# Where the activations of a two-layer trunk lie in SBUF, and a paired up product in its first network

## The chip, the cores and the metric

The kernel runs on one core of a Trainium2 chip. The metric is the device time of one execution in microseconds, the median of several runs. All arithmetic is in 32-bit floats; large products split each operand into a high part, rounded to the format that TensorE multiplies in one pass (float32r), and a low part, the rest.

## The reference

A sequence of 256 tokens of width 2048 goes through two layers. Each layer is a token mixer and a gated network; each sub-layer is normalised, scaled and shifted by a modulation computed from a vector c, and added back through a gate.

```python
for i in range(DEPTH):
    shift, scale, gate = ada_ln(c, mix_mod_w[i], mix_mod_b[i])
    h = rms_norm(x, mix_norm_g[i]) * (1.0 + scale) + shift
    y = conformer_conv_module(h, ...) if i % 2 == 0 else stick_breaking_mixer(h, ...)
    x = x + gate * y
    shift, scale, gate = ada_ln(c, ffn_mod_w[i], ffn_mod_b[i])
    h = rms_norm(x, ffn_norm_g[i]) * (1.0 + scale) + shift
    x = x + gate * conv_ffn(h, ffn_up_w[i], ffn_dw_w[i], ffn_dw_b[i], ffn_down_w[i])
return rms_norm(x, final_norm_g)

def conv_ffn(h, up_w, dw_w, dw_b, down_w):
    u = causal_depthwise_conv(h @ up_w, dw_w, dw_b)   # width 3, 2 x 5632 channels
    gt, val = jnp.split(u, 2, axis=-1)
    return (jax.nn.silu(gt) * val) @ down_w
```

## The kernel before

Everything is kept transposed: channels on the 128 partitions, the 256 tokens along the free axis. A width of 2048 is thus 16 tiles of 128 x 256, the network's 5632 channels are 44. A product runs over weight blocks of 128 x 128; a column block (128 output channels) of an up product has 16 weight blocks, one of a down product 22 in each of its two halves. Eight weight blocks are a piece of 512 KB, loaded by SyncE's queue. For each piece ScalarE casts the weights to the high part `wh` (line 244) and VectorE subtracts to the low part `wl` (line 248). `look["split"]` is 3: this is done three pieces ahead of the piece that TensorE works on; `wh` and `wl` have four buffers each, `raw` six.

`gemm` (line 271 on) multiplies in one of two ways. Without `both`, a weight block takes three matmuls of 256 columns: `wh` by the operand's high half (304), `wh` by its low half (305), `wl` by its high half (306). With `both` it takes two: `wh` by high and low half together, 512 columns (299), and `wl` by the high half, 256 columns (300). The first of these leaves two partial sums side by side in PSUM, and whoever takes the result must add the halves.

The stages in order: convolution mixer (products pw1, pw2), first network (up00a, up00b, up01a, down00, up01b, down01), attention (qk, v, o), second network (the same names with a 1 first), final norm. A network's up product is cut in two halves, each followed by a down product over the 22 tiles that it has made; up00a, qk0a and up10a are the four column blocks with which a stage opens, on an operand that is not yet normalised, and never paired. Before the change, the products up10b, up11a, up11b, the later query and key products, all down products (but one column block each) and o are paired; up00b, up01a, up01b are not.

`up_done` takes each finished column block of an up product to `conv3`: ScalarE makes y, the last tap with its bias (line 1000), VectorE adds the two earlier taps (1003). With `both`, ScalarE first copies one half from PSUM (996) and VectorE adds the other (997). When gate and value of a channel tile are there, ScalarE takes the silu (1014), VectorE multiplies (1015), ScalarE casts the result to g's high half (1017), VectorE subtracts to its low half (1018). In `down_done` ScalarE scales one half (1024), GpSimd adds it to x (1025) and VectorE adds the other half (1029).

Beside the products runs the modulation. Rows of the modulation weights are loaded by GpSimd's queue (331) and reduced against silu(c) by VectorE (338). `tick`, called after each piece, spreads these steps by `RATES`: 0.4 a piece in up00b, 0.39 in the other up products of the first network, 0.43 in the down products. `Entry.add` scales x into a raw h as soon as a column block of x is done (458, 459), and `Rms.add` adds up squares, on GpSimd (406).

Tiles lie in SBUF in the order of their pools: constants, x, the 16 tiles of h, weight buffers, temporaries, modulation rows, and last what belongs to a stage (the convolution's tiles, z, g, or attention's with o). An h tile holds two halves of 264 floats (2112 bytes); the first h tile begins at byte 32,800 of each partition, which is 32 modulo 256. A g tile has 2304 bytes, its low half 1056 bytes behind the high one, and begins at 160 modulo 256; an o tile has 2176 bytes, so the o tiles begin at 160 and 32 in turn.

Of the kernel before, what the change touches and what calls it, by code (L numbers as in the profile page):

```python
# [26 lines left out]

PAIRS = {"z": (264, 528, 0), "g0": (264, 576, 0), "g1": (264, 576, 0), "o": (264, 544, 0)}
HEAD = 16
# [88 lines left out]
def hybrid_trunk(ctx: ExitStack, tc: tile.TileContext, cfg: Cfg, io: dict):  # L118
    nc = tc.nc
    D, T, H = cfg.D, cfg.T, cfg.H  # L120
    KD, KF, CW, FW = cfg.KD, cfg.KF, cfg.CW, cfg.FW
# [22 lines left out]
    def t256(name="t", bufs=6):  # L144
        return tmp.tile([P, T], F32, name=name, bufs=bufs)
# [10 lines left out]
    nc.vector.memset(ones_d, 1.0 / D)  # L156
    ones_q = const.tile([P, P], F32, name="ones_q")
    nc.vector.memset(ones_q, 1.0 / 32)
    ones = const.tile([P, P], F32, name="ones")
    nc.vector.memset(ones, 1.0)  # L160
    eps_r = const.tile([P, 1], F32, name="eps_r")
# [16 lines left out]
    fill = []  # L178
# [185 lines left out]
    HP = T + 8  # L364
    pairs = {}

    def h_tiles(i):
        v = hpool.tile([P, 2 * HP], F32R, name=f"h{i}")
        pairs[i] = v.rearrange("p (a t) -> p a t", a=2)[:, :, :T]
        return [v[:, a * HP:a * HP + T + 2] for a in range(2)]  # L370

    def h_pairs():
        return [pairs[k] for k in range(KD)]

    ahead_of = {kind: v[2] for kind, v in PAIRS.items()}

    def halved(pool, kind, name):

        low, size, _ = PAIRS[kind]
        at = ahead_of.pop(kind, 0)  # L380
        v = pool.tile([P, at + size], F32R, name=name)[:, at:at + 2 * low].rearrange("p (a t) -> p a t", a=2)[:, :, :T]
        return v[:, 0], v[:, 1], v
# [122 lines left out]
    with ExitStack() as cv:  # L505
# [12 lines left out]
        for k in range(0, D, 512):  # L518
            ps = psum_acc()
            nc.tensor.matmul(ps, ones[0:1, :], crow[0:1, k:k + 512], start=True, stop=True)  # L520
            nc.scalar.activation(csr[:, k:k + 512], ps, AF.Silu)
        rs = rms.rstd()
# [127 lines left out]
        for kt in range(KD):  # L650
# [5 lines left out]
        ident = homes_of_taps.pop()  # L656
        nc.gpsimd.affine_select(out=ident, in_=ones, pattern=[[1, P]], compare_op=ALU.is_equal, fill=0.0, base=0,
                                channel_multiplier=-1)
# [123 lines left out]
        def gather_copy(name):  # L782
            st["g" + name] = t256()
            nc.scalar.copy(st["g" + name], st[name][:, :T])

        def gather(name):

            nc.tensor.matmul(st[name][:, T:2 * T], ones_q, st.pop("g" + name), start=True, stop=name == "y0",
                             skip_group_check=True)
# [191 lines left out]
    def ffn(i, entry, out):  # L981
# [3 lines left out]
        with ExitStack() as fs:  # L985
# [6 lines left out]
            def conv3(ps, nb, both):  # L992
                y = t256()
                if both:
                    s = t256()
                    nc.scalar.copy(s, ps[:, T:2 * T])
                    nc.vector.tensor_tensor(s, ps[:, :T], s, op=ALU.add)
                    ps = s
# [90 lines left out]
    with ExitStack() as at:  # L1089
# [9 lines left out]
        ones_r = apool.tile([P, P], F32R, name="ones_r")  # L1099
        nc.scalar.copy(ones_r, ones)  # L1100

# [259 lines left out]
```

## Time and profile before

| | |
|---|---|
| median of 3 runs | 2296.48 us (2296.34 to 2298.68) |
| profiled execution | 2295.19 us |
| span of its instructions | 2293.5 us |
| granted TensorE clock | 0.998 |
| VectorE busy | 1790.7 us, 78% |
| ScalarE busy | 1218.8 us, 53% |
| GpSimd busy | 410.7 us, 18% |

The profile is of one execution. Its page gives the busy time of each engine, the clock in 40 slices, the chain of work that ended last, and the costliest groups of instructions; a group reads "line, engine, operation, output<-inputs, shapes, count | busy us, mean ns of one | idle us of the engine before them, and what ended it". The trace behind it can be asked for the same groups within a window, for busy time by window, for waits, and for instructions in order of time (start, duration, what). Matmuls overlap and their ends are modelled, so the time of one is read from the length of a stage divided by the number of its weight blocks.

### The profile page before, as it was taken

Reading aid. Unit: us, or ns where it says so; the run is one execution under the profiler, and the core shown is the slowest. Engines: PE = TensorE matmul, PEld = TensorE weight load, DVE = VectorE, ACT = ScalarE, POOL = GpSimd, SP = SyncE. Lnnn points to the kernel's source line nnn. Section 1 sums busy time; section 2 is a strip of 40 time slices with the busy share of each in tenths; the row PEclk is TensorE's granted clock in tenths of the full one; section 3 lists DMA queues with packets and bytes.
Section 4 is the critical chain, followed back from the end, with each engine's and each line's share of the span. In section 5 each row is a group of like instructions: output and inputs, shape, how many; then the busy total and the mean of one; then the engine's idle time right before and its main releaser. Section 6 shows DMA issues by size and latency. Waiting matters only on the chain.

```text
span 2293.5 us, 37839 instructions
## 1 busy us (share of the span) xinstructions
PE 2259.2 (99%) x14466; PEld 2011.7 (88%) x14466; DVE 1790.7 (78%) x2504; ACT 1218.8 (53%) x1930; POOL 410.7 (18%) x534
## 2 busy tenths in 40 slices
PE   7999999999999999999999999999999999999997
PEld 5888678999998999998898888888888888888887
DVE  7689968989998899999975555779899755777654
ACT  2056655755544455554465555657555544555553
POOL 4058713200003100003411100112000010000031
PEclk9999999999999999999999999999999999999999
DMA  9988798789899989888755555566777566656663
GB/s 397 417 336 305 273 363 349 290 298 337 332 350 340 338 329 340 336 333 307 277 185 159 165 174 169 170 189 235 240 282 277 193 191 188 190 185 186 192 192 111
DMA packets 139144, 603.16 MB, mean 263 GB/s; under 512 B 15441, under 2 KB 15569, under 8 KB 115153
## 3 DMA queue, kind: packets, MB, share of 16 engines
q1 hardware_dynamic: 120242, 464.42, 57.7%
q0 software_dynamic: 18720, 136.32, 16.0%
q8 instruction: 113, 1.85, 0.3%
q14 instruction: 69, 0.57, 0.1%
HBM read 598.58 MB, written 2.10 MB: 262 GB/s over the span
## 4 chain that ended last, share of the span: by engine, by line
PE 86%; DVE 7%; DMA 4%; ACT 1%; issue 1%; POOL 0%; DVEq 0%; SPq 0%; ACTq 0%; POOLq 0%
PE ps L299 32%; PE ps L300 16%; PE ps L304 9%; PE ps L305 9%; PE ps L306 8%; PE ps L694 5%; DMA mraw<-in_mt_mix 3%; DVE mraw L338 3%; DVE wl L248 2%; PE ps L1184 1%; PE ps L1185 1%; PE ps L1186 1%; PE ps L586 1%; DMA mraw<-in_mt_ffn 1%; DMA raw<-in_w_pw 1%
## 5 line engine op out<-in xcount | busy, mean ns | idle before, releaser
L248 DVE TENSOR_TENSOR wl<-raw,wh 128x1024 fp32r<-128x1024 f32 x688 | 848.0, 1239 | 299.5 <-ACT wh L244 297.7
L244 ACT CAST wh<-raw 128x1024 fp32r<-128x1024 f32 x688 | 719.0, 1047 | 660.6 <-PE ps L299 283.5
L299 PE MATMUL ps<-h,wh 128*128 128x512 f32 x1760 | 619.0, 394 | 0.0
L300 PE MATMUL ps<-h,wl 128*128 128x256 f32 x1760 | 494.0, 281 | 0.0
L299 PE MATMUL ps<-g,wh 128*128 128x512 f32 x1320 | 458.6, 393 | 0.0
L304 PE MATMUL ps<-h,wh 128*128 128x256 f32 (+1 forms) x1504 | 422.0, 281 | 0.0
L305 PE MATMUL ps<-h,wh 128*128 128x256 f32 (+1 forms) x1504 | 420.8, 280 | 0.0
L306 PE MATMUL ps<-h,wl 128*128 128x256 f32 (+1 forms) x1504 | 419.2, 279 | 0.1
L299 PEld LDWEIGHTS ps<-h,wh 128*128 128x128 f32 x1760 | 330.5, 188 | 74.5
L338 DVE CUSTOM_DVE_ANT_0 mraw<-mraw,csr 128x2048 f32<-128x2048 f32 x152 | 350.4, 2305 | 31.2 <-DMA mraw<-in_mt_mix 28.5
L300 PE MATMUL ps<-g,wl 128*128 128x256 f32 x1320 | 367.8, 279 | 2.3 <-DVE wl L248 2.2
L300 PEld LDWEIGHTS ps<-h,wl 128*128 128x128 f32 x1760 | 332.7, 189 | 0.2
L299 PEld LDWEIGHTS ps<-g,wh 128*128 128x128 f32 x1320 | 247.8, 188 | 57.8
L305 PEld LDWEIGHTS ps<-h,wh 128*128 128x128 f32 x1504 | 284.8, 189 | 0.1
L306 PEld LDWEIGHTS ps<-h,wl 128*128 128x128 f32 x1504 | 282.8, 188 | 0.7 <-DVE wl L248 0.7
L304 PEld LDWEIGHTS ps<-h,wh 128*128 128x128 f32 x1504 | 282.6, 188 | 0.1
L300 PEld LDWEIGHTS ps<-g,wl 128*128 128x128 f32 x1320 | 248.1, 188 | 4.1 <-DVE wl L248 4.1
L694 PE MATMUL ps<-h,raw 128*128 128x256 f32 x832 | 188.6, 382 | 0.0
L694 PEld LDWEIGHTS ps<-h,raw 128*128 128x128 f32 x832 | 158.0, 191 | 28.1 <-issue 5.8
L1025 POOL TENSOR_TENSOR x<-x,t 128x256 f32<-128x256 f32 x56 | 70.0, 1250 | 530.1 <-ACT t L1024 529.8
L1003 DVE SCALAR_TENSOR_TENSOR t<-t,par 128x254 f32<-128x254 f32 (+1 forms) x184 | 88.8, 483 | 46.6 <-ACT t L1000 43.7
L734 DVE SCALAR_TENSOR_TENSOR auxb<-u,cpar,auxb 128x256 f32<-128x256 f32 x297 | 121.6, 483 | 4.5 <-ACT auxb L718 3.7
(272 smaller groups left out, 2735.0 us busy)
## 6 DMA issues: line engine op xcount, KB each, us to landing
raw<-in_w_down SPq DMA_DIRECT2D x176, 512.0 KB, 4.3
mraw<-in_mt_ffn POOLq DMA_DIRECT2D x64, 1024.0 KB, 6.7
raw<-in_w_pw SPq DMA_DIRECT2D x96, 512.0 KB, 8.0
mraw<-in_mt_mix POOLq DMA_DIRECT2D x48, 1024.0 KB, 7.9
raw<-in_w_up01b SPq DMA_DIRECT2D x84, 512.0 KB, 6.8
raw<-in_w_up11b SPq DMA_DIRECT2D x84, 512.0 KB, 3.6
raw<-in_w_up00b SPq DMA_DIRECT2D x80, 512.0 KB, 6.1
raw<-in_w_up10b SPq DMA_DIRECT2D x80, 512.0 KB, 4.7
```

Source lines behind the costliest of these rows:

```text
L244: nc.scalar.copy(wh[:, :n], v[:, :n])
L248: nc.vector.tensor_tensor(wl[:, :n], v[:, :n], wh[:, :n].bitcast(F32), op=ALU.subtract)
L299: nc.tensor.matmul(o, wh[:, c], both[kt], start=first, stop=False, skip_group_check=True)
L300: nc.tensor.matmul(o[:, :T], wl[:, c], xh[kt], start=False, stop=left[nb] == 0, skip_group_check=True)
L304: nc.tensor.matmul(o, wh[:, c], xh[kt], start=first, stop=False, skip_group_check=halves > 0)
L305: nc.tensor.matmul(o, wh[:, c], xl[kt], start=False, stop=False, skip_group_check=halves > 0)
L306: nc.tensor.matmul(o, wl[:, c], xh[kt], start=False, stop=left[nb] == 0, skip_group_check=halves > 0)
L338: nc.vector.tensor_tensor_reduce(out=v, in0=v, in1=csr, scale=1.0, scalar=0.0, op0=ALU.mult, op1=ALU.add, accum_out=macc[:, nb:nb + 1])
L694: nc.tensor.matmul(banks[j][:, nb // KD * T:(nb // KD + 1) * T], w[:, b * P:(b + 1) * P], hf[kt], start=first, stop=left[j] == 0, skip_gro ...
L734: nc.vector.scalar_tensor_tensor(conv_ps[j], us[j % UBUFS][:, k:k + T], tap(j, k), conv_ps[j], op0=ALU.mult, op1=ALU.add)
L1003: nc.vector.scalar_tensor_tensor(y[:, s:], ps[:, :T - s], w(k), y[:, s:], op0=ALU.mult, op1=ALU.add)
L1025: nc.gpsimd.tensor_tensor(xs[nb], xs[nb], t, op=ALU.add)
```

## The change

- **h.** An h tile gets 2304 bytes (the last one 2176), and the first begins 128 bytes later. With the constants 1024 bytes shorter, the first h then begins at byte 31,904 and all of them at 160 modulo 256, their low halves still 1056 bytes further.
- **g of the first network, and o.** Halves of 1024 bytes without a gap, so that the 512 columns are one run; all of them begin at 64 modulo 256. The second network's g stays as it was.
- **The first network's up product** is paired, as the second's is. ScalarE copies all 512 columns of a finished block from PSUM to a new tile `e`, GpSimd adds the halves there, and y and the two taps read the sum from SBUF.
- **Room.** The constants 1/32 and 1 go: ScalarE multiplies by D or D/32 in operations that it already had, and GpSimd fills the identity with ones itself. The two tiles m1 and dm of the convolution take the slots of the temporaries `tm`.

```diff
-PAIRS = {"z": (264, 528, 0), "g0": (264, 576, 0), "g1": (264, 576, 0), "o": (264, 544, 0)}
+PAIRS = {"z": (264, 528, 0), "g0": (256, 512, 40), "g1": (264, 576, 0), "o": (256, 512, 40)}
+H_AHEAD, H_SIZE, H_LOW, H_LAST = 32, 576, 264, 544
...
-    ones_q = const.tile([P, P], F32, name="ones_q")
-    nc.vector.memset(ones_q, 1.0 / 32)
-    ones = const.tile([P, P], F32, name="ones")
-    nc.vector.memset(ones, 1.0)
...
     def h_tiles(i):
-        v = hpool.tile([P, 2 * HP], F32R, name=f"h{i}")
-        pairs[i] = v.rearrange("p (a t) -> p a t", a=2)[:, :, :T]
-        return [v[:, a * HP:a * HP + T + 2] for a in range(2)]
+        at = H_AHEAD if i == 0 else 0
+        v = hpool.tile([P, at + (H_LAST if i == KD - 1 else H_SIZE)], F32R, name=f"h{i}")
+        pairs[i] = bass.AP(tensor=v.tensor, offset=v.offset + at, ap=[list(v.ap[0]), [H_LOW, 2], [1, T]])
+        return [v[:, at + a * H_LOW:at + a * H_LOW + T + 2] for a in range(2)]
...
-        low, size, _ = PAIRS[kind]
-        at = ahead_of.pop(kind, 0)
-        v = pool.tile([P, at + size], F32R, name=name)[:, at:at + 2 * low].rearrange("p (a t) -> p a t", a=2)[:, :, :T]
+        low, size, ahead = PAIRS[kind]
+        at = ahead if foremost.setdefault(kind, name) == name else 0
+        v = pool.tile([P, at + size], F32R, name=name)
+        v = bass.AP(tensor=v.tensor, offset=v.offset + at, ap=[list(v.ap[0]), [low, 2], [1, T]])
         return v[:, 0], v[:, 1], v
...
-            nc.tensor.matmul(ps, ones[0:1, :], crow[0:1, k:k + 512], start=True, stop=True)
-            nc.scalar.activation(csr[:, k:k + 512], ps, AF.Silu)
+            nc.tensor.matmul(ps, ones_d[0:1, :], crow[0:1, k:k + 512], start=True, stop=True)
+            nc.scalar.activation(csr[:, k:k + 512], ps, AF.Silu, scale=float(D))
...
-        nc.gpsimd.affine_select(out=ident, in_=ones, pattern=[[1, P]], compare_op=ALU.is_equal, fill=0.0, base=0,
+        nc.gpsimd.memset(ident, 1.0)
+        nc.gpsimd.affine_select(out=ident, in_=ident, pattern=[[1, P]], compare_op=ALU.is_equal, fill=0.0, base=0,
...
-        m1 = cpool2.tile([P, T], F32, name="m1")
-        dm = cpool.tile([P, T], F32, name="dm")
+        m1 = t256("tm", 2)
+        dm = t256("tm", 2)
...
             def conv3(ps, nb, both):
                 y = t256()
-                if both:
+                if both and i == 0:
+                    s = gpool.tile([P, 2 * T], F32, name="e", bufs=2)
+                    nc.scalar.copy(s, ps)
+                    nc.gpsimd.tensor_tensor(s[:, :T], s[:, :T], s[:, T:], op=ALU.add)
+                    ps = s
+                elif both:
                     s = t256()
                     nc.scalar.copy(s, ps[:, T:2 * T])
                     nc.vector.tensor_tensor(s, ps[:, :T], s, op=ALU.add)
...
-            both = h_pairs() if i else None
-            rest = (lambda nb, ps: up_done(nb, ps, True)) if i else up_done
+            both = h_pairs()
+            rest = lambda nb, ps: up_done(nb, ps, True)
```

More of the change, by code (lines that the diff above doesn't have):

```diff
@@ L367, in h_tiles @@
     def h_tiles(i):
-        v = hpool.tile([P, 2 * HP], F32R, name=f"h{i}")
-        pairs[i] = v.rearrange("p (a t) -> p a t", a=2)[:, :, :T]
-        return [v[:, a * HP:a * HP + T + 2] for a in range(2)]
+        at = H_AHEAD if i == 0 else 0
+        v = hpool.tile([P, at + (H_LAST if i == KD - 1 else H_SIZE)], F32R, name=f"h{i}")
+        pairs[i] = bass.AP(tensor=v.tensor, offset=v.offset + at, ap=[list(v.ap[0]), [H_LOW, 2], [1, T]])
+        return [v[:, at + a * H_LOW:at + a * H_LOW + T + 2] for a in range(2)]
     def h_pairs():
         return [pairs[k] for k in range(KD)]
-    ahead_of = {kind: v[2] for kind, v in PAIRS.items()}
+    foremost = {}
     def halved(pool, kind, name):
-        low, size, _ = PAIRS[kind]
-        at = ahead_of.pop(kind, 0)
-        v = pool.tile([P, at + size], F32R, name=name)[:, at:at + 2 * low].rearrange("p (a t) -> p a t", a=2)[:, :, :T]
+        low, size, ahead = PAIRS[kind]
+        at = ahead if foremost.setdefault(kind, name) == name else 0
+        v = pool.tile([P, at + size], F32R, name=name)
+        v = bass.AP(tensor=v.tensor, offset=v.offset + at, ap=[list(v.ap[0]), [low, 2], [1, T]])
         return v[:, 0], v[:, 1], v
@@ L783, in gather_copy @@
             st["g" + name] = t256()
-            nc.scalar.copy(st["g" + name], st[name][:, :T])
+            nc.scalar.activation(st["g" + name], st[name][:, :T], AF.Copy, scale=D / 32.0)
         def gather(name):
-            nc.tensor.matmul(st[name][:, T:2 * T], ones_q, st.pop("g" + name), start=True, stop=name == "y0",
+            nc.tensor.matmul(st[name][:, T:2 * T], ones_d, st.pop("g" + name), start=True, stop=name == "y0",
                              skip_group_check=True)
@@ L1099, in hybrid_trunk @@
         ones_r = apool.tile([P, P], F32R, name="ones_r")
-        nc.scalar.copy(ones_r, ones)
+        nc.scalar.activation(ones_r, ones_d, AF.Copy, scale=float(D))
         def attention(h):
```

## The prediction

> **What bounds the kernel now.** I read the page's busy shares, clock and chain first, to see which engine sets the end.
>
> ```profile
> span 2293.5 us, 37839 instructions
> PE 2259.2 (99%) x14466; PEld 2011.7 (88%) x14466; DVE 1790.7 (78%) x2504; ACT 1218.8 (53%) x1930; POOL 410.7 (18%) x534
> PEclk9999999999999999999999999999999999999999
> PE 86%; DVE 7%; DMA 4%; ACT 1%; issue 1%; POOL 0%; DVEq 0%; SPq 0%; ACTq 0%; POOLq 0%
> ```
>
> TensorE is busy nearly all the time, at full clock, and is 86% of the chain. Two things can therefore move the end: the time of a matmul, and a weight that arrives late. So next I cut the span into the two networks' product stages (columns: length, then busy time and count of PE, weight loads, VectorE, ScalarE, GpSimd, then clock and DMA).
>
> ```profile
> 429.70:665.70 236.00, 235.60 (x2018) 235.40 (x2018) 219.69 (x293) 127.80 (x182) 15.18 (x29) 1.00 0.89 335
> 665.70:780.10 114.40, 114.40 (x663) 99.85 (x662) 98.08 (x98) 50.91 (x59) 28.25 (x32) 1.00 0.93 348
> 780.10:787.90 7.80, 7.80 (x69) 7.80 (x68) 6.58 (x7) 2.53 (x3) 0.53 (x1) 1.00 1.01 392
> 787.90:1023.10 235.20, 235.20 (x2019) 235.20 (x2018) 216.50 (x275) 123.21 (x180) 16.41 (x31) 1.00 0.89 332
> 1023.10:1141.80 118.70, 116.41 (x663) 100.36 (x662) 113.47 (x125) 60.37 (x90) 44.59 (x40) 1.00 0.81 295
> 1923.20:2158.40 235.20, 235.20 (x1347) 206.31 (x1346) 169.01 (x248) 133.63 (x206) 0.00 (x0) 1.00 0.61 188
> 2158.40:2272.80 114.40, 114.40 (x662) 99.86 (x661) 58.62 (x60) 62.48 (x88) 27.79 (x27) 1.00 0.55 167
> ```
>
> Rows 1 and 4 are the first network's up product (42 column blocks of 16 weight blocks each: 672), three matmuls of 256 columns per weight block. Row 6 is the second network's up product: 672 weight blocks too, but two matmuls, one of 512 columns and one of 256. Both take 235.2 us, 350.0 ns a weight block. **Pairing by itself saves no TensorE time.** Row 7 is a down product, also paired: 330 weight blocks in 114.4 us, 346.7 ns. The same two matmuls are 3.3 ns cheaper on g than on h.
>
> What differs is where the operand lies. Counting the tiles up as they are allocated, every g begins at byte 160 modulo 256 with its low half at 192. An h tile is 2112 bytes, so the h tiles begin in turn at 32, 96, 160 and 224 modulo 256. After the change every h begins at 160 with its low half at 192: the places that g has now.
>
> Unpaired, those places look no better: row 3 is a column block of g with three matmuls, 22 weight blocks in 7.8 us, 355 ns against 350 for h unpaired.
>
> **VectorE is the second limit in the first network only.** In rows 1 and 4 it is idle for 236.0 - 219.69 = 16.3 us and 235.2 - 216.50 = 18.7 us, together 35.0. In row 5, the second down product, it is at 113.47 of 118.7, and there TensorE needs 4.3 us more than the 114.4 of its siblings. The waits of that stage say on what:
>
> ```profile
> PEld ps L300 <- DVE wl L248: 4.1, 6, 1.0
> ```
>
> So a VectorE that is nearly full costs TensorE time, through the low halves of the weights.
>
> **The change, part by part.**
>
> *Placement of h.* Paired products on h gain 3.3 ns a weight block, taken from rows 6 and 7. Second network: 2 x 672 = 1344 blocks, 4.5 us. Attention's paired query and key products: 28 column blocks x 16 = 448, 1.5 us. The three stages that open on unpaired h (12 column blocks, 192 weight blocks) may lose as row 3 suggests: 192 x 5 ns = 0.9 at most, 0 at least; I take 0.5.
>
> *Pairing up 0.* 1344 blocks go from 350.0 to 346.7 ns: 4.5 us of TensorE time, if the weights keep up.
>
> *g of the first network and o.* They get halves of exactly 1024 bytes, one run of 512, beginning at 64 modulo 256. No operand of the trace has that place in a run of its own. The nearest rows are 6 and 7: between 346.7 and 350 ns, and not beyond, as both contain mixed and uniform places. With 660 paired blocks of g and 256 of o, that is 0 to 3 us of loss; a gain can't be excluded, since nothing shows that 160 is the best of all places: the same 3 us the other way. I take 0.
>
> *What follows a finished column block (84 times).* ScalarE copies 512 columns from PSUM, GpSimd adds the halves, ScalarE makes y from SBUF, VectorE's two taps read SBUF instead of PSUM.
>
> ```profile
> L1190 ACT COPY v<-ps 128x512 f32<-128x512 f32 x6 | 3.5, 587 | 4.1 <-PE ps L1186 3.7
> L1000 ACT ACTIVATE t<-t,par 128x256 f32<-128x256 f32 x92 | 55.3, 601 | 89.2 <-DVE t L997 89.1
> L1000 ACT ACTIVATE t<-ps,par 128x256 f32<-128x256 f32 x82 | 45.8, 558 | 0.0
> L1003 DVE SCALAR_TENSOR_TENSOR t<-t,par 128x254 f32<-128x254 f32 x92 | 44.3, 482 | 43.7 <-ACT t L1000 43.7
> L1003 DVE SCALAR_TENSOR_TENSOR t<-ps,par,t 128x254 f32<-128x254 f32 x82 | 39.1, 477 | 0.0
> L734 DVE SCALAR_TENSOR_TENSOR auxb<-u,cpar,auxb 128x256 f32<-128x256 f32 x297 | 121.6, 483 | 4.5 <-ACT auxb L718 3.7
> L869 POOL TENSOR_TENSOR y<-y,h 128x256 f32<-128x256 f32 x143 | 104.7, 732 | 13.3 <-ACT h L743 3.2
> L1025 POOL TENSOR_TENSOR x<-x,t 128x256 f32<-128x256 f32 x56 | 70.0, 1250 | 530.1 <-ACT t L1024 529.8
> ```
>
> ScalarE gets 84 x (587 + 601 - 558) = 53 us more on 251 busy of 471: it has room. VectorE's own operations stay as they are (482 against 477). GpSimd gets 84 adds of 0.73 us (L869) to 1.25 us (L1025), 61 to 105 us of 471, almost unused now. None of that is on the path by itself. The price is what the add does to VectorE:
>
> ```profile
> 719.97 1.78 POOL L1025 TENSOR_TENSOR x<-x,t 128x256 f32<-128x256 f32 x1 [2.36 <-ACT t L1024]
> 718.87 2.29 DVE L338 CUSTOM_DVE_ANT_0 mraw<-mraw,csr 128x2048 f32<-128x2048 f32 x1
> 721.08 1.75 DVE L248 TENSOR_TENSOR wl<-raw,wh 128x1024 fp32r<-128x1024 f32 x1
> ```
>
> The add starts inside L338, lasts 1.78 us instead of 0.73, and ends at 721.75; the split that VectorE starts at 721.08 takes 1.75 instead of 1.21 to 1.22. They take turns: the add waits for the running VectorE operation, and the next one waits 0.54 us for the add. It is not so for every pair: the adds of L869 run beside the convolution taps of L734, which have one operand in SBUF and one in PSUM, and neither is stretched (732 and 483). Split, reduction, product and, after the change, the taps of up 0 all read two operands from SBUF.
>
> The Trainium skill ("SBUF — State Buffer", Who interferes with whom) states this as a rule: a VectorE instruction with two SBUF inputs contends with a GpSimd one that reads SBUF, one with a single SBUF input does not. "Perfetto Trace Analysis" of the same skill (Optimizing Scalar/DVE Operations) warns that moving work between the two might not help. The trace agrees with the first; the second would come out as the first rival below.
>
> How often it happens is read from the same groups in stages with and without adds (first half of up 0, down 0, down 1, in this order):
>
> ```profile
> L248 DVE TENSOR_TENSOR wl<-raw,wh 128x1024 fp32r<-128x1024 f32 x85 | 102.9, 1221 | 13.8 <-ACT wh L244 13.1
> L338 DVE CUSTOM_DVE_ANT_0 mraw<-mraw,csr 128x2048 f32<-128x2048 f32 x29 | 66.2, 2284 | 0.0
> L248 DVE TENSOR_TENSOR wl<-raw,wh 128x1024 fp32r<-128x1024 f32 x42 | 52.8, 1271 | 9.9 <-ACT wh L244 9.9
> L338 DVE CUSTOM_DVE_ANT_0 mraw<-mraw,csr 128x2048 f32<-128x2048 f32 x18 | 41.8, 2322 | 0.0
> L248 DVE TENSOR_TENSOR wl<-raw,wh 128x1024 fp32r<-128x1024 f32 x42 | 57.4, 1378 | 2.2 <-ACT wh L244 2.2
> L338 DVE CUSTOM_DVE_ANT_0 mraw<-mraw,csr 128x2048 f32<-128x2048 f32 x17 | 39.7, 2338 | 0.0
> L459 DVE SCALAR_TENSOR_TENSOR h<-x,a_mix,h 128x256 fp32r<-128x256 f32 x14 | 12.5, 894 | 1.8 <-ACT h L458 1.8
> L1025 POOL TENSOR_TENSOR x<-x,t 128x256 f32<-128x256 f32 x14 | 22.5, 1605 | 22.1 <-ACT t L1024 22.0
> L406 POOL TENSOR_TENSOR sumsq<-sumsq,t 128x256 f32<-128x256 f32 x13 | 15.4, 1186 | 35.9 <-ACT t L402 35.9
> ```
>
> Down 0, VectorE 86% busy: 42 x 0.050 + 18 x 0.038 = 2.8 us over 14 adds, 0.20 us each. Down 1, 96% busy: 42 x 0.157 + 17 x 0.054 + 14 x (0.894 - 0.48) = 13.3 us over 27 adds, 0.49 us each. Up 0 stands at 93% before the adds, so it is nearest to the second: 84 x 0.49 = 41 us (17 and 45 are the ends, by 0.20 and by 0.54), against 35.0 us of idle time and 4.5 us less TensorE time. VectorE would come out 41 - 35 + 4.5 = 10.7 us too slow, about 5 us in each half.
>
> That is about what the pipeline can hide. A weight piece is split three pieces ahead, 8 blocks x 0.35 x 3 = 8.4 us; cast (row below) and subtraction take 1.05 and 1.22 of it, so VectorE can be some 6 us late. The lag of the first half is worked off in down 0 (114.4 - 98.08 = 16 us idle). That of the second enters down 1, which has 5.2 us idle and loses time already. I charge 2 us in up 0 (0 to the 17.5 of the rival) and 3 us in down 1 (0 to 5).
>
> ```profile
> L244 ACT CAST wh<-raw 128x1024 fp32r<-128x1024 f32 x688 | 719.0, 1047 | 660.6 <-PE ps L299 283.5
> ```
>
> *New waits.* ScalarE's y waits for the add, up to one VectorE operation of 2.3 us plus 0.73. Behind it stands the cast of the next piece, and behind that VectorE's subtraction; the 6 us of cover serve here too. The add in turn stands in GpSimd's queue behind the loads of modulation rows, which wait for the buffer that a reduction frees:
>
> ```profile
> POOL mraw L331 <- DVE macc L338: 70.6, 11, 13.9
> ```
>
> That buffer was reduced a step earlier in VectorE's order, so I cost it at nothing; if VectorE lags by a step, it is the rival's mechanism too. The removed constants, the rescaled ones, the identity's memset and m1 and dm in other slots lie beside stages that wait for transfers and reductions: 0.
>
> *Sum.* -4.5 - 1.5 + 0.5 - 4.5 + 0 + 2 + 3 = -5.0 us. The profiled execution took 2295.19, its span 2293.5 and 1.7 around it; that gives 2290.2. The median of the runs is 1.3 above the profiled one: 2291.5.
>
> **The rivals.**
>
> *VectorE becomes the bound (slower).* Each block's chain (copy, add that waits for VectorE, y, taps) leaves VectorE idle as well as locked out. For: down 1 shows 4.3 us lost per 114.4 with VectorE at 96%. Against: down 1 also carries h and the squares. Price: 4.3 x 471/114.4 = 17.7 us in up 0 in place of 2, so +11: 2307. It decides once an add costs VectorE over 0.14 us more than 0.49 (6 us of cover over 42 blocks).
>
> *The adds land in VectorE's idle time (faster).* For: the splits of row 1 wait 13.1 us for casts, and the add comes just behind a cast. At 0.20 us each, 17 us fit into 35. Then the 5 us of stalls go: 2286.5.
>
> *Placement does nothing.* The change would not do what it says: h's 350 ns comes from something else than its address, say the traffic of VectorE and ScalarE in those stages. Against: row 6 and row 7 differ although their VectorE shares are both low (72% and 51%), and row 1 gives 350 with another load. Then the gains of 10 are 0; VectorE is only 41 - 35 = 6 us too slow, and half of the stalls stays: 2299. The Trainium skill ("SBUF — State Buffer", Who interferes with whom) has TensorE never wait on anyone and names no rule of place; that is this case, and the 3.3 ns between g and h speak against it.
>
> **How the numbers follow.** About 0.2% is what a measurement here can tell from no change, 4.6 us. Forecast 0.40, its share on the faster side 0.25, within 0.15 (2291.5 lies at the bound); VectorE the bound 0.28, slower; adds hidden 0.15, faster; placement nothing 0.17, of it 0.13 within and 0.04 slower. Faster 0.40, same 0.28, slower 0.32. The range reaches from the hidden adds with a gain at g (2285) to VectorE as the bound (2308). As both signs hold much, the forecast's own range is 2288 to 2296.
>
> **What would show it.** Second network's up product: 232.9 to 233.1 us instead of 235.2; 235 says placement does nothing. First network's: 233 to 237 instead of 235.2 and 236.0, with VectorE over 98% busy, splits near 1.4 us and GpSimd adds of 1.1 to 1.8. Down 1: 119 to 124 instead of 118.7. If up 0 takes over 240 a half, with TensorE waiting for L248, the rival has it; if splits stay at 1.25, the adds are hidden.

## The result and the profile after

The changed kernel takes 2316.95 us (median of 4 runs, 2314.52 to 2318.45) against 2296.41 (4 runs, 2296.07 to 2298.68) measured beside it: a ratio of 1.0086, 95% interval 1.0073 to 1.0099. It is slower by 20.5 us, and outside the range that was given. Of e2, e3 and e10 below, one execution each ran at a granted clock of 0.66 to 0.85 and took 2475 us or more; without it the medians given there would be lower by 0.2, 0.2 and 0.8 us.

The profiled execution took 2317.71 us. Its page, for the whole span:

```profile
span 2316.0 us, 35321 instructions
PE 2263.1 (98%) x13122; PEld 1948.3 (84%) x13122; DVE 1819.8 (79%) x2502; ACT 1252.3 (54%) x2014; POOL 554.8 (24%) x619
PE 72%; DVE 16%; DMA 4%; issue 4%; ACT 2%; POOL 1%; DVEq 0%; SPq 0%; ACTq 0%; POOLq 0%
```

TensorE's share of the chain fell from 86% to 72%, VectorE's rose from 7% to 16%: the end now waits for VectorE in places. Where, the cut into stages says (columns as in the prediction; first and second half of the first network's up product, its two down products, then the two halves of the second network's up product):

```profile
433.20:679.40 246.20, 237.89 (x1346) 203.68 (x1345) 229.42 (x288) 143.44 (x221) 84.64 (x72) 1.00 0.88 315
803.20:1048.90 245.70, 237.83 (x1345) 203.44 (x1345) 227.00 (x268) 136.76 (x205) 85.93 (x73) 1.00 0.87 310
679.40:795.50 116.10, 114.75 (x663) 101.47 (x662) 103.29 (x103) 52.69 (x62) 32.01 (x35) 1.00 0.95 354
1048.90:1170.10 121.20, 117.62 (x663) 102.63 (x662) 117.75 (x132) 63.15 (x107) 48.14 (x42) 0.99 0.82 302
1592.00:1825.80 233.80, 233.25 (x1346) 203.46 (x1345) 209.43 (x309) 140.53 (x223) 6.88 (x13) 1.00 0.75 263
1948.00:2180.90 232.90, 232.90 (x1346) 203.31 (x1345) 168.91 (x248) 133.50 (x206) 0.00 (x0) 1.00 0.60 190
```

The second network gained what was expected: 232.9 us where it was 235.2, 346.6 ns a weight block. The first network's up product lost 10.2 and 10.5 us (246.2 and 245.7, from 236.0 and 235.2). Of the span's 22.5 us, up 0 makes 20.7, the two down products 1.7 and 2.5, the stages before the first network 3.5 (2.6 of it a drop of the clock, see the last section); the second network and the attention give 5.4 back (the remaining -0.5 is spread over the rest).

The waits of the second half of up 0 (engine, who waited on whom: us in all, times, longest):

```profile
ACT t L1005 <- POOL e L997: 63.4, 33, 2.5
ACT g L1022 <- DVE t L1020: 40.2, 20, 4.2
PEld ps L297 <- DVE wl L245: 13.6, 20, 1.5
PE ps L297 <- DVE wl L245: 7.7, 9, 1.2
DVE t L1008 <- ACT t L1005: 8.8, 7, 1.3
DVE wl L245 <- ACT wh L241: 6.6, 6, 1.6
```

TensorE waits for VectorE's low halves (third and fourth row). ScalarE stands for 63 us with y until GpSimd's add is there, and VectorE waits for ScalarE in the last two rows. Before the change ScalarE's casts waited for TensorE in this half, 71 times and for 94.3 us in all: it was ahead, now it is behind.

```profile
ACT wh L244 <- PE ps L305: 94.3, 71, 1.8
```

The groups of the first half show what the add does to VectorE (last, the second tap of the kernel before, over both halves):

```profile
L245 DVE TENSOR_TENSOR wl<-raw,wh 128x1024 fp32r<-128x1024 f32 x84 | 107.8, 1298 | 3.0 <-ACT wh L241 3.0
L997 POOL TENSOR_TENSOR e<-e 128x256 f32<-128x256 f32 x41 | 70.0, 1706 | 163.3 <-ACT e L996 128.9 <-issue 34.4
L335 DVE CUSTOM_DVE_ANT_0 mraw<-mraw,csr 128x2048 f32<-128x2048 f32 x28 | 64.4, 2301 | 0.0
L1008 DVE SCALAR_TENSOR_TENSOR t<-e,par,t 128x255 f32<-128x255 f32 x40 | 26.4, 659 | 0.9
L1008 DVE SCALAR_TENSOR_TENSOR t<-e,par,t 128x254 f32<-128x254 f32 x40 | 19.0, 475 | 10.5 <-ACT t L1005 10.5
...
L1003 DVE SCALAR_TENSOR_TENSOR t<-ps,par,t 128x255 f32<-128x255 f32 x82 | 39.4, 481 | 1.5
```

The splits take 1298 ns instead of 1221, the second tap of each block (255 columns) 659 instead of 481, the reductions 2301 instead of 2284: 84 x 0.077 + 40 x 0.178 + 28 x 0.017 = 14.1 us that VectorE stands still in this half for 41 adds. (Op by op the sum is 14.5; the table below has it so. I call it the lost time.) And one place, in order of time, shows both effects in a row:

```profile
581.77 2.29 DVE L335 CUSTOM_DVE_ANT_0 mraw<-mraw,csr 128x2048 f32<-128x2048 f32 x1
582.41 2.25 POOL L997 TENSOR_TENSOR e<-e 128x256 f32<-128x256 f32 x1 [3.71 <-issue]
583.98 1.75 DVE L245 TENSOR_TENSOR wl<-raw,wh 128x1024 fp32r<-128x1024 f32 x1
584.69 0.60 ACT L1005 ACTIVATE t<-e,par 128x256 f32<-128x256 f32 x1 [2.43 <-POOL e L997]
585.20 1.98 ACT L241 CAST wh<-raw 128x1024 fp32r<-128x1024 f32 x2
```

The add arrives inside a reduction and ends 0.6 us after it; the split that follows is drawn out to 1.75 us; ScalarE has idled 2.43 us with y, and the cast of the next piece stands behind that y.

### The profile page after: what moved, and what is told of

The parts are those of the page before. It is cut to its first block, busy times and chain, and to the rows that moved or that the text cites. A ratio compares the mean times of both kernels' runs of the same rounds, so it can differ in the third digit from the quotient of the medians.

```text
span 2316.0 us, 35321 instructions
## 1 busy us (share of the span) xinstructions
PE 2263.1 (98%) x13122; PEld 1948.3 (84%) x13122; DVE 1819.8 (79%) x2502; ACT 1252.3 (54%) x2014; POOL 554.8 (24%) x619
## 4 chain that ended last, share of the span: by engine, by line
PE 72%; DVE 16%; DMA 4%; issue 4%; ACT 2%; POOL 1%; DVEq 0%; SPq 0%; ACTq 0%; POOLq 0%
PE ps L296 36%; PE ps L297 18%; DVE wl L245 6%; DVE mraw L335 5%; PE ps L694 5%; DMA mraw<-in_mt_mix 3%; PE ps L301 2%; PE ps L302 2%; DVE t L1008 2%; PE ps L303 2%; PE ps L1190 1%; PE ps L1189 1%; PE ps L1191 1%; ACT wh L241 1%; PE ps L585 1%
## 5 line engine op out<-in xcount | busy, mean ns | idle before, releaser
L296 PE MATMUL ps<-h,wh 128*128 128x512 f32 x3072 | 1070.8, 394 | 0.0
L297 PE MATMUL ps<-h,wl 128*128 128x256 f32 x3072 | 857.6, 279 | 15.6 <-DVE wl L245 15.3
L296 PEld LDWEIGHTS ps<-h,wh 128*128 128x128 f32 x3072 | 576.7, 188 | 132.3
L297 PEld LDWEIGHTS ps<-h,wl 128*128 128x128 f32 x3072 | 576.8, 188 | 26.7 <-DVE wl L245 26.6
L335 DVE CUSTOM_DVE_ANT_0 mraw<-mraw,csr 128x2048 f32<-128x2048 f32 x152 | 349.8, 2301 | 31.6 <-DMA mraw<-in_mt_mix 29.5
L997 POOL TENSOR_TENSOR e<-e 128x256 f32<-128x256 f32 x84 | 142.9, 1702 | 338.1 <-ACT e L996 269.0
L1005 ACT ACTIVATE t<-e,par 128x256 f32<-128x256 f32 x84 | 50.6, 602 | 135.8 <-POOL e L997 135.8
L1008 DVE SCALAR_TENSOR_TENSOR t<-e,par,t 128x254 f32<-128x254 f32 (+1 forms) x168 | 95.3, 567 | 21.1 <-ACT t L1005 19.4
L869 POOL TENSOR_TENSOR y<-y,h 128x256 f32<-128x256 f32 x143 | 104.4, 730 | 13.3 <-ACT h L743 3.2
L1005 ACT ACTIVATE t<-t,par 128x256 f32<-128x256 f32 x92 | 55.3, 601 | 89.6 <-DVE t L1002 89.5
L405 POOL TENSOR_TENSOR sumsq<-sumsq,t 128x256 f32<-128x256 f32 x56 | 64.8, 1158 | 154.4 <-ACT t L401 154.4
```

Source lines behind the costliest of these rows:

```text
L296: nc.tensor.matmul(o, wh[:, c], both[kt], start=first, stop=False, skip_group_check=True)
L297: nc.tensor.matmul(o[:, :T], wl[:, c], xh[kt], start=False, stop=left[nb] == 0, skip_group_check=True)
L335: nc.vector.tensor_tensor_reduce(out=v, in0=v, in1=csr, scale=1.0, scalar=0.0, op0=ALU.mult, op1=ALU.add, accum_out=macc[:, nb:nb + 1])
L869: nc.gpsimd.tensor_tensor(ys[c], ys[c], pr, op=ALU.add)
L997: nc.gpsimd.tensor_tensor(s[:, :T], s[:, :T], s[:, T:], op=ALU.add)
L1005: nc.scalar.activation(y, ps[:, :T], AF.Identity, bias=pc(f"fdb{i}", nb, 1), scale=w(FW - 1))
```

## The experiments

Two things were added at the same spot: time lost by VectorE to the add, and a wait of ScalarE (with its casts behind it) for the add. Two theories were tried first: queue theory, by which ScalarE's queue, held up by the wait, sets the length of up 0, and lock theory, by which VectorE does, through the lost time. Later runs ask whether it takes the two together. The rival was the new placement. All medians are compared with the kernel before on the same chip, 2296.4 to 2296.6 us in the three groups of runs.

This table collects up 0 of the profiles (e1 and e3 are given in the text), first half / second half, in us: length, VectorE busy (union over the window), idle (length less busy), and lost time (each op's duration over its value in the kernel before).

| kernel | length | busy | idle | lost | median |
|---|---|---|---|---|---|
| before | 236.0 / 235.2 | 219.7 / 216.5 | 16.3 / 18.7 | 0.1 / 0.1 | 2296.41 |
| after | 246.2 / 245.7 | 229.4 / 227.0 | 16.8 / 18.7 | 14.5 / 15.0 | 2316.95 |
| e2 VectorE adds | 233.8 / 233.0 | 228.3 / 225.8 | 5.5 / 7.2 | 0.1 / 0.1 | 2287.58 |
| e4 idle add, unpaired | 238.3 / 237.4 | 230.2 / 227.8 | 8.1 / 9.6 | 10.9 / 11.4 | 2294.38 |
| e5 no add | 233.8 / 233.0 | 218.6 / 215.7 | 15.2 / 17.3 | 0.1 / 0.2 | 2288.38 (one run) |
| e6 y later | 242.1 / 240.1 | 234.2 / 232.4 | 7.9 / 7.7 | 19.1 / 20.0 | 2304.21 |
| e7 hold only | 233.8 / 232.9 | 218.1 / 214.9 | 15.7 / 18.0 | 0.1 / 0.1 | 2286.58 |
| e8 lost time only | 241.1 / 240.7 | 232.6 / 230.4 | 8.5 / 10.3 | 18.3 / 19.2 | 2308.47 |
| e9 both, apart | 243.1 / 242.0 | 232.9 / 231.8 | 10.2 / 10.2 | 16.3 / 18.0 | 2307.72 |
| e10 full VectorE, idle add | 241.7 / 242.6 | 239.3 / 236.3 | 2.4 / 6.3 | 12.3 / 11.6 | 2306.12 |
| e11 a tap less | 233.1 / 233.0 | 214.0 / 212.7 | 19.1 / 20.3 | 15.1 / 15.5 | 2287.18 |

### The placement alone (e1)

The changed kernel with up 0 unpaired, as before:

```diff
-            both = h_pairs()
-            rest = lambda nb, ps: up_done(nb, ps, True)
+            both = h_pairs() if i else None
+            rest = (lambda nb, ps: up_done(nb, ps, True)) if i else up_done
```

> The changed kernel with the first network's up product unpaired again, as before; the places of h, g and o stay changed. Queue theory (ScalarE's queue, held up by y's that wait for GpSimd's add, paces up 0) and lock theory (VectorE, held up by the adds in the shared port, paces it): no adds, so no stalls; the second network and attention keep their gain of 5.4 us, up 0 takes between 235 (place indifferent to unpaired matmuls) and 238 us a half (355 ns a weight block, as g unpaired): 2291 to 2297 us. If the new places themselves cost the time: 2310 or more.

Measured: 2295.01 us, ratio 0.9994 (0.9984 to 1.0003). The second network's up halves take 233.7 and 233.0, as after. But unpaired up 0 takes 237.4 us in its second half instead of 235.2, 353 ns a block, and the first half 238.1, 2.1 more (VectorE idle for 18.0 and 20.5 us): three matmuls on h are slower at the new places, as the row of g unpaired (355 ns) had suggested. So the placement isn't what costs 20 us, and it pays only together with pairing.

### VectorE adds the halves (e2)

The first network goes the second network's way: ScalarE copies one half from PSUM, VectorE adds the other from PSUM. GpSimd has no add.

```diff
-                if both and i == 0:
-                    s = gpool.tile([P, 2 * T], F32, name="e", bufs=2)
-                    nc.scalar.copy(s, ps)
-                    nc.gpsimd.tensor_tensor(s[:, :T], s[:, :T], s[:, T:], op=ALU.add)
-                    ps = s
-                elif both:
+                if both:
```

> The changed kernel with the halves added by VectorE straight from PSUM, as the second network does it, and ScalarE copying one half only. Queue theory: y waits for an add of 0.42 us that stands in VectorE's own queue instead of one that waits for VectorE; ScalarE waits 30 to 40 us a half instead of 66, and the casts keep up: up 0 234 to 238 us a half, 2289 to 2297 us. Lock theory: 84 adds of 0.335 us, 28 us, in place of the 28 us by which the lock stretched VectorE's operations: no better than the changed kernel, 2308 to 2317.

Measured: 2287.58 us, ratio 0.9963 (0.9948 to 0.9977); it beats both kernels. Queue theory's forecast is nearly met, lock theory's isn't.

```profile
431.90:665.70 233.80, 233.26 (x1347) 203.38 (x1346) 228.30 (x331) 139.90 (x223) 14.76 (x28) 1.00 0.90 334
787.80:1020.80 233.00, 233.00 (x1347) 203.40 (x1346) 225.81 (x312) 134.62 (x221) 16.47 (x31) 1.00 0.89 330
```

VectorE is 97 to 98% busy and TensorE loses nothing. The add costs VectorE 9.7 and 10.1 us a half more busy time than without any add (e5); the first of these windows holds one reduction of 2.3 us less than e5's, so I count 10 to 12. Left to GpSimd it costs VectorE 14.5 to 15.0 us in after and 18.3 to 19.2 in e8: the move took more from VectorE than it gave.

### The wait moved later (e3, e6)

In e3 the steps behind the add (y, taps, and what follows) were issued one piece later in the program:

```diff
+            def finish_aged():
+                with tc.high_priority(offset=PRIORITY):
+                    while aged:
+                        up_done(*aged.pop(0), True)
+                aged.extend(fresh)
+                fresh.clear()
+                tick()
```

> The changed kernel, with copy and add where they are, but y, the two taps and what follows them issued one weight piece (2.8 us) later, so that ScalarE need not stand and wait for the add. The adds and the lock stay. Queue theory: ScalarE's waits for the add fall from 66 to under 20 us a half, up 0 takes 234 to 238, the kernel 2290 to 2299. Lock theory: VectorE loses as much as before, up 0 stays at 244 to 247, the kernel at 2312 to 2318.

Measured: 2320.66 us, ratio 1.0104 (1.0083 to 1.0124). It says nothing on the wait: ScalarE waited 72 us for the adds in the second half, as before (63), so the later issue didn't take the wait away (that half took 248.4 us). In e6 the steps came two pieces later, with y ordered behind the last cast:

```diff
         nc.scalar.copy(wh[:, :n], v[:, :n])
+        look["cast"] = list(nc.cur_bb.bb.instructions)[-1]
...
+                if both and i == 0:
+                    behind(look["cast"])
...
+            ages = [[], [], []]
```

> The changed kernel with y, the taps and what follows issued two weight pieces (5.6 us) after copy and add, and y put behind the cast that was last issued, so that copy and y no longer stand side by side in ScalarE's queue (69 of 84 do in the changed kernel, 1 of 84 here). The adds and the lock stay. Queue theory: ScalarE's waits for the add fall from 66 us a half to under 15, up 0 takes 234 to 238 us a half, the kernel 2288 to 2298. Lock theory: no change, 2312 to 2320.

Measured: 2304.21 us, ratio 1.0036 (1.0023 to 1.0049), 12.7 us below after. The waits of its second half:

```profile
ACT g L1042 <- DVE t L1040: 66.1, 19, 5.4
ACT wh L241 <- PE ps L297: 24.1, 24, 1.8
PEld ps L298 <- DVE wl L246: 6.9, 12, 1.2
```

Nearly all of y's waits for the add are gone, ScalarE's casts wait for TensorE again, and VectorE's idle time falls to 8 us a half. Yet it loses 19 to 20 us to the add and TensorE still waits for it. Neither theory's forecast is met: the wait is a part of the loss, not all of it.

### No add, and a hold without an add (e5, e7)

e5 is the changed kernel without GpSimd's add: y goes on with the lower half alone, the second partial sum is left out.

```diff
-                    nc.gpsimd.tensor_tensor(s[:, :T], s[:, :T], s[:, T:], op=ALU.add)
```

> The changed kernel without the GpSimd add: the second partial sum (high weights by low activations) is left out of up 0, ScalarE still copies all 512 columns, and y reads the first half at once. Every theory but one that blames the copy or the places: no waits, up 0 233 to 234 us a half, about 2285 us.

Measured, one run: 2288.38 us, halves of 233.8 and 233.0. The rest of the change (the copy of 512, y and taps from SBUF) costs nothing in up 0: e2 and e7 have the same halves. In e7 three GpSimd memsets stand in the add's place, so that y waits as long but nothing takes VectorE's reads; it sets the block's result to zero. Casts are ordered behind the last y, so that ScalarE's queue keeps its order:

```diff
+        if "y" in look:
+            behind(look["y"])
...
-                    nc.gpsimd.tensor_tensor(s[:, :T], s[:, :T], s[:, T:], op=ALU.add)
+                    for _ in range(3):
+                        nc.gpsimd.memset(s, 0.0)
```

> The changed kernel with three GpSimd memsets of the 512 columns in place of each add (about 1.6 us together; up 0's result is set to zero, so the product is left out of the output), and the casts kept behind y: ScalarE stands and waits as long as in the changed kernel, but nothing that GpSimd does there reads SBUF. Queue theory: the stall stays without the lock, up 0 242 to 247 us a half, 2306 to 2318. Lock theory: VectorE's operations are no longer stretched and up 0 takes 233 to 236, 2284 to 2291.

Measured: 2286.58 us, ratio 0.9966 (0.9957 to 0.9976). Its waits in the second half, and its second half:

```profile
ACT t L1008 <- POOL e L1000: 67.6, 38, 1.8
```

```profile
786.30:1019.20 232.90, 232.90 (x1345) 203.30 (x1345) 214.90 (x276) 142.10 (x218) 81.69 (x155) 1.00 0.91 329
```

ScalarE stands for 67.6 us, more than after the change (63.4), with its casts behind; TensorE doesn't notice. That is lock theory's forecast, and against queue theory's: the wait alone is free.

### The lost time alone (e4, e8)

e4 takes e1 and adds, per block, a ScalarE copy and a GpSimd add whose result nobody reads:

```diff
+                es = [gpool.tile([P, 2 * T], F32, name=f"e{k}") for k in range(2)]
...
+                if i == 0:
+                    es.append(es.pop(0))
+                    nc.scalar.copy(es[0][:, :T], ps[:, :T])
+                    nc.gpsimd.tensor_tensor(es[0][:, :T], es[0][:, :T], es[0][:, T:], op=ALU.add)
+                up_done(nb, ps, bool(i))
```

> The placed kernel with an unpaired up 0, and beside it, for each of the 84 column blocks, a ScalarE copy of 256 columns and a GpSimd add of the same size as the changed kernel's whose result nobody reads. It measures the lock alone. Queue theory: nobody waits for the add, so 0 to 4 us over the placed kernel without it. Lock theory: VectorE loses the same 28 us, up 0 comes to 244 or more a half, 15 to 25 us over it.

Measured: 2294.38 us, ratio 0.9991 (0.9982 to 1.0). No cost, and on this run alone the lost time would have been cleared. But it is unpaired: TensorE's half is 4.5 us longer there, and the lost time is 11 us, not 15 to 19. About 10 of these 11 us came out of VectorE's idle time (from 18.0 and 20.5 in e1 to 8.1 and 9.6): part of it was room. So it was put to the test again with pairing. In e8 the add is after's, except that its sum goes over the upper half, which nobody reads; y goes on with the lower half at once:

```diff
-                    nc.gpsimd.tensor_tensor(s[:, :T], s[:, :T], s[:, T:], op=ALU.add)
+                    nc.gpsimd.tensor_tensor(s[:, T:], s[:, T:], s[:, :T], op=ALU.add)
```

> The changed kernel with the sum of GpSimd's add written over the upper half of e, which nobody reads: the first network's up product stays paired, ScalarE copies both halves, GpSimd adds in the same place and for as long, but y and the taps go on with the lower half alone (the second partial sum is left out) as soon as the copy is done. So VectorE still loses the time that GpSimd's add takes from it, at the short paired TensorE time of 233 us a half, and nothing waits for the add. Theory A (the lost time alone: 219 us of work and 15 us of stretch are more than TensorE's 233 leaves): the halves of up 0 stay near 243 to 246 us, 2309 to 2316 us in all. Theory B (it takes the lost time and the wait of y for the add together): halves of 233 to 236, VectorE's ops still stretched by 10 to 15 us, its idle time down from 15-18 to 3-8, 2287 to 2293 us.

Measured: 2308.47 us, ratio 1.0055 (1.004 to 1.007). Windows of its halves, and waits of the second:

```profile
433.90:675.00 241.10, 237.01 (x1346) 204.16 (x1345) 232.62 (x288) 148.40 (x223) 79.06 (x72) 1.00 0.89 321
798.70:1039.40 240.70, 237.40 (x1346) 204.13 (x1345) 230.38 (x268) 140.36 (x205) 81.14 (x73) 1.00 0.88 317
```

```profile
ACT g L1022 <- DVE t L1020: 58.6, 20, 4.5
ACT wh L241 <- PE ps L296: 21.9, 23, 1.7
ACT t L1019 <- DVE t L1008: 18.2, 11, 3.1
PEld ps L297 <- DVE wl L245: 7.5, 14, 1.0
DVE wl L245 <- ACT wh L241: 7.0, 7, 1.6
PE ps L297 <- DVE wl L245: 3.2, 7, 0.7
```

ScalarE no longer waits for the add, part of its casts wait for TensorE again, and still each half is 7.3 to 7.7 us longer than in e5. The only difference to e5 is the add itself: it costs 2308.47 - 2288.38 = 20.1 us (15.0 in up 0, 4.3 in the two down products, of which 1.7 is a drop of the clock). The same rows of e5 show what the lost time does to ScalarE:

```profile
ACT wh L241 <- PE ps L296: 76.5, 77, 1.8
DVE wl L245 <- ACT wh L241: 13.4, 13, 1.6
ACT g L1021 <- DVE t L1019: 7.2, 6, 1.9
```

Without the add ScalarE waits for TensorE, and for VectorE's product only 7.2 us. With it, it waits for VectorE's product and second tap (58.6 + 18.2 us), and its casts stand behind these waits; so VectorE, late itself, still waits 7.0 us for casts. The forecast of theory B, 2287 to 2293, was wrong; theory A's 2309 to 2316 was nearly met. What after has on top, 2316.95 - 2308.47 = 8.5 us, is y's wait for the add: VectorE's idle time goes from 8.5 and 10.3 back to 16.8 and 18.7.

### Hold and lost time, apart (e9)

e7 with one more GpSimd add behind the memsets, which nobody waits for:

```diff
                     for _ in range(3):
                         nc.gpsimd.memset(s, 0.0)
+                    nc.gpsimd.tensor_tensor(s[:, T:], s[:, T:], s[:, :T], op=ALU.add)
```

> The kernel with the memsets in the add's place (y waits behind them some 67 us a half, which by itself cost nothing), and behind them a GpSimd add that nobody waits for. ScalarE's hold and VectorE's stretch are both there, but what ScalarE waits for is not itself drawn out by VectorE. As there, the halves' values are set to zero. Theory B1 (any hold of ScalarE's queue and the stretch add up): halves near 243 to 246, 2309 to 2316 us. Theory B2 (only the add that is itself drawn out by VectorE, while VectorE waits for y, closes the ring): halves of 233 to 237, 2287 to 2295 us.

Measured: 2307.72 us, ratio 1.0048 (1.0033 to 1.0063), halves of 243.1 and 242.0. Theory B1's number is nearly met, but not its idea: e9 is as long as e8, which has no hold, and 9 us short of after. A hold of fixed length adds little to the lost time (1.3 to 2.0 us a half, and nothing in the total). What is left for the last 8.5 us is that the add which y waits for is itself held up by VectorE; that is a conclusion from the difference, not a run of its own.

### A full VectorE, and a lighter one (e10, e11)

e10 is e2 with a ScalarE copy of 256 and a GpSimd add per block that nobody reads:

```diff
                 if both:
+                    if i == 0:
+                        d = gpool.tile([P, T], F32, name="d")
+                        nc.scalar.copy(d, ps[:, T:2 * T])
+                        nc.gpsimd.tensor_tensor(d, d, d, op=ALU.add)
                     s = t256()
```

> The kernel in which VectorE adds the halves (2287.6 us, VectorE busy for 228 of 233 us, idle for 5 to 8), with one ScalarE copy of 256 and one GpSimd add of 256 per block that nobody reads. The lock takes some 10 to 15 us a half from a VectorE that has 5 to 8 us to give, and ScalarE waits for nobody's add. If VectorE's time is a bound of its own: halves of 237 to 244, VectorE idle under 4 us, 2296 to 2312 us. If the lost time costs only where ScalarE waits for the add: halves of 233 to 234.5, 2287 to 2291 us.

Measured: 2306.12 us, ratio 1.0042 (1.0029 to 1.0056): some 18 us above e2.

```profile
433.20:674.90 241.70, 236.24 (x1347) 203.72 (x1346) 239.32 (x330) 151.46 (x264) 74.31 (x72) 1.00 0.87 323
797.00:1039.60 242.60, 236.94 (x1346) 203.91 (x1345) 236.32 (x309) 146.69 (x262) 74.86 (x73) 1.00 0.86 315
```

Here VectorE is idle for 2.4 us of 241.7: a full engine, which the lost 12 us a half push past TensorE. Then e11, the changed kernel with one of VectorE's two taps left out in the first network:

```diff
-                for k in range(FW - 1):
+                for k in range(FW - 1 if i else 1):
```

> The changed kernel with the second of the two taps of the first network's convolution left out (some 41 ops of 0.48 us to 0.58 us a half less on VectorE, 20 to 24 us), the add and ScalarE's wait for it kept. If VectorE's work is a link of what sets the time: halves of 233 to 237, 2288 to 2296 us. If the wait of ScalarE for the add sets it whatever VectorE has to do: halves of 241 to 246, 2305 to 2316 us.

Measured: 2287.18 us, ratio 0.9965 (0.9955 to 0.9974).

```profile
431.40:664.50 233.10, 233.10 (x1346) 203.45 (x1345) 213.96 (x246) 145.33 (x223) 72.59 (x73) 1.00 0.91 335
786.60:1019.60 233.00, 233.00 (x1347) 203.49 (x1346) 212.73 (x233) 138.50 (x213) 71.72 (x73) 1.00 0.90 328
```

The add, ScalarE's wait for it (53.3 us in the second half) and the lost time of 15 us a half are all still there, and the whole loss is gone. So in the changed kernel VectorE's work is a link of what sets the length of up 0. A tap less also shortens the way from y to the silu, which this run doesn't separate; e10 needs no such way to lose its 18 us. (The profiled execution took 2292.54 us, 5.4 above the median; the excess lies in the second network, see the last section.)

## Why the prediction was wrong

**Placement: right.** The second network gave 2.2 and 2.3 us, the 4.5 forecast; the attention 0.9 instead of 1.5 (274.6 to 273.7). The unpaired openings of the stages cost nothing instead of 0.5: the last 144 matmuls of each take 17.8 us before and after. g of the first network and o at their new places changed nothing (in e1 down 0 takes 114.4 us as before, down 1 118.3 against 118.7; o takes 72.4 us before and after). The rival in which placement does nothing is out.

**Pairing up 0: right.** e2 and e5 show 233.8 and 233.0 instead of 236.0 and 235.2: 4.4 us. (The prediction's "Both take 235.2 us" holds for row 4; row 1 takes 236.0.)

**The price of an add: the size was too high.** 0.49 us was taken; after's halves lose 14.5 and 15.0 us over 41 adds each, 0.35 to 0.37 us an add, e8's 0.45 to 0.47. Over 84 adds that is 30 us in after, not 41.

**The step that failed is the next one: "84 x 0.49 = 41 us ... against 35.0 us of idle time".** It took all of VectorE's idle time as room. Only a part of it is: some 10 us a half in e4, 7 in e8, none in after. With a loss of 30 us instead of 41, 35.0 of room less the 4.4 by which TensorE got shorter should have been enough; instead after has 16.8 and 18.7 us of idle time in its halves, as much as before (16.3 and 18.7), and the lost time went straight into the length. From e5 to after, first half: 14.5 us lost, 1.6 more idle, together 16.1, of which 12.4 are in the length. In e8, where ScalarE doesn't wait for the add, 18.3 are lost, 6.7 are taken from the idle time, and 7.3 of the other 11.6 are in the length. VectorE's idle time is made of waits for ScalarE (8.8 + 6.6 of the 18.7 us in after's second half, by the waits above), and ScalarE is late when VectorE is (76.8 us of waits for VectorE in e8's second half, 7.2 in e5's). In the kernels that lost time and had no wait for the add, 2 to 10 us a half stayed.

**The cover of "some 6 us": right in kind.** The parts that are not in the length, 16.1 - 12.4 = 3.7 and 11.6 - 7.3 = 4.3 us, are the lag with which VectorE leaves the half: the windows of both kernels hold one split, one reduction and two taps fewer than e5's. It shows in time, too. TensorE's groups in after, for the first 67 us of up 0 and then for the rest of the half:

```profile
L297 PE MATMUL ps<-h,wl 128*128 128x256 f32 x159 | 44.1, 278 | 0.0
...
L297 PE MATMUL ps<-h,wl 128*128 128x256 f32 x482 | 136.0, 282 | 7.8 <-DVE wl L245 7.6
```

For 67 us TensorE has no wait but one of 0.5 at the very start; then the cover is used up, and the waits for VectorE begin. The cover pays once; a shortage pays per block.

**"The 6 us of cover serve here too": wrong.** The new wait of ScalarE was costed with the same cover, so at nothing of its own. By itself it is nothing (e7). On top of the lost time it costs 8.5 us (after against e8), when the cover is already used up: the add waits for VectorE's running operation, ScalarE for the add, the next cast for ScalarE, and VectorE for the cast.

**Down 1: 3 forecast, 2.5 measured.** 1.7 of it is a drop of the clock, below; it follows a pause of 1.8 us in which TensorE waits for a split, where the longest such wait before was 0.7. Down 0 took 1.7 where the lag was to be worked off for nothing.

**The rival "VectorE becomes the bound" was the case,** by its place and by its sign that TensorE would wait for the split in halves of over 240 us. Its price of 17.7 us for up 0 (17.5 where the charge of 2 us is given its bounds, a slip) was short of 25.1 (246.2 + 245.7 less 233.8 and 233.0); the lost time alone makes 15.0 of these (e8), the wait for the add the other 10.1. Its point of decision was wrong: it was to need adds of over 0.63 us and came with 0.36, for the same reason as the forecast failed. "VectorE over 98% busy", the sign of the forecast itself, says little either: after's VectorE is busy for 92 to 93% of up 0 and sets its length, e2's for 97 to 98% and doesn't.

The Trainium skill ("Perfetto Trace Analysis", Optimizing Scalar/DVE Operations) warns that offloading between VectorE and GpSimd might not help as they share a read port. The runs agree and give it a size: 10 to 12 us a half for the add on VectorE, 14.5 to 19.2 us lost to it on GpSimd (after and e8).

## What to carry to other kernels

An engine's idle time is room only as far as it does not consist of waits for a neighbour that the change delays too: before spending it, ask which waits make it up and whether they would go if the engine were late. Work moved from VectorE to GpSimd is priced in VectorE's time, both for its turns and for whoever waits for the moved operation, and a fixed cover in pieces hides a lag once, not a shortage per block. And an experiment that clears a cost clears it only at the margin at which it ran: the add that nobody waits for cost nothing in e4, where TensorE's half is 4.5 us longer and VectorE lost 11 us, and 20 us in e8.

## What the runs showed of the hardware

**The clock drops after a short pause.** At the end of the product before the first network TensorE waits for a small copy, 1.8 us in after and 1.6 before. Windows of after: up to the drop, in it, behind it; then a pause in down 1, where TensorE waits 1.8 us for a split, and the drop behind it (the column before the last two is the granted clock):

```profile
394.00:397.90 3.90, 2.09 (x14) 1.88 (x12) 3.90 (x5) 3.41 (x6) 0.00 (x0) 0.84 1.01 414
397.90:403.00 5.10, 5.10 (x25) 5.10 (x25) 5.10 (x13) 2.04 (x9) 1.12 (x1) 0.50 1.02 409
403.00:408.90 5.90, 5.90 (x50) 5.90 (x50) 4.67 (x15) 4.00 (x14) 1.39 (x1) 0.96 0.64 223
...
1093.00:1096.40 3.40, 1.61 (x10) 1.17 (x9) 2.77 (x4) 1.83 (x4) 2.29 (x4) 1.00 0.08 33
1096.40:1099.80 3.40, 3.40 (x12) 2.85 (x11) 3.40 (x3) 1.23 (x2) 1.12 (x2) 0.50 0.91 328
```

The last 72 matmuls of that product take 11.1 us in after, 8.5 before; among the experiments they take 8.5 (e7, e11), 10.1 (most) or 11.1 to 11.3 (e5, e8). The granted clock stands at half for no time, for 3.4 and for 6.8 us in these three groups (6.8 in after), and the second drop, of 3.4 us, costs 1.7 us (after and e8 have it). The length of the pause doesn't decide: e4 pauses for 1.59 us and drops, e7 for 1.75 and doesn't. So 2.6 of after's profiled 22.5 us come from the first drop and not from the change's mechanism; the second follows a wait for VectorE and may be owed to the change. The Trainium skill ("TensorE: Matmul & The Clock Gate", HAM oscillation) gives the rule to leave no idle gap of over about 3.4 us, after which TensorE is throttled; the gaps here are 1.6 to 1.8 us. What decides at such a gap isn't shown.

**The place of the operand counts by shape.** 512 and 256 columns on h cost 350.0 ns a block at mixed places and 346.6 with all tiles at 160 modulo 256; three times 256 columns cost 350.0 at the mixed places and 353 at 160 (e1). Why this is so isn't shown. And the place isn't all: in e11's profiled execution the second network's first up half and the down product behind it took 238.1 and 116.6 us instead of 233.8 and 114.4 in after, 353 to 354 ns a block, at the same places and a granted clock of 1.00; its second half was back at 346.7. What slowed that stretch is open.

**The turns are not of fixed price.** GpSimd adds of one size, 41 a half, took 1.14 us on average (e6, second half) to 1.71 (after), and cost VectorE 0.27 (e4) to 0.49 us each (e6); e6 and after have the same operations in another order.
